# A two-layer streaming trunk on one core: gating values moved ahead of the pooling and kept in DRAM, system stores moved from ACT to SP

## The chip, the core and the metric

The kernel runs on one core of a Trainium2 chip, in one launch. A core has a matrix engine (TensorE, PE in the profile), a vector engine (VectorE, DVE), an activation engine (ScalarE, ACT), a general engine (GpSimd, POOL) and a sync engine (SyncE, SP), each with its own instruction stream that runs in order; they meet at semaphores. SP and ACT issue the transfers here. The metric is the device time of one execution in microseconds (us); lower is better.

## What is computed

Two layers with the same structure, for a prompt of 1024 tokens and eight sample requests of 16 tokens, 1152 tokens in all. In each layer one projection of the normalised tokens feeds four branches of 256 channels, and the gated branches go through an output projection that is added to the tokens:

```
x <- x + W_out[ silu(gates) * concat(A, B, C, D) ]      (all inputs from W_in @ rmsnorm(x))
A: time mixing   s = s*w_t + (s @ -kk_t)(kk_t*a_t) + v_t k_t ;  y_t = s @ r_t     (4 heads of 64)
B: latent attention with a rotary key and a block-causal mask
C: u * (W_s @ layer_norm(v) + b), W_s lower triangular, over chunks of 128 positions
D: trailing means over windows of 2, 4, 8, 16, minus the token, a linear map per group
```

The normalised v of the sample tokens (branch C) is one of the outputs, vn_o.

## The kernel before

The tokens stand in three groups of 384 columns. A layer is a row of projection blocks of 128 output channels: 24 for the inputs (F_ORDER) and 8 for the output. One block is 72 matmuls of 128x128 by 128x384: for each token group, eight parts of the input times three products (each factor is split into a high and a low part, xh, xl and wh, wl). The names in F_ORDER are the blocks: WDAD, K, R, V feed branch A, D and GD the pooling and its gate, VC and U the gating branch's values and inputs, GC its gate, Q, Q1K, CK the attention, GB and GA the other gates. Index 0 or 1 is the half of the 256 channels.

The weights of a block come in four pieces of 128 KB, issued by SP (line 238, wr, three buffers), copied to a high part by ACT (241) and a low part by POOL (242), in eight buffers each, so the weights of one block are made while the block before it runs. Each group's result lies in one of two pj buffers of PSUM until a sink on ACT and DVE has taken it (lines 383 to 400 for the blocks of branch A: scale, shift by one token, and for the third group the last columns into sho).

Beside the blocks run lanes: generators that put their instructions between the block's matmuls at fixed places (tick). Lane a holds the time mixing. For each half and token group, elementwise work gives keys and decays (kb, ar; 437 to 494). systems() (506 to 519) makes for each of 18 chunks of 64 tokens a triangular system: eight small matmuls into b, a mask on DVE into one of two ns buffers, and a store to DRAM (517). The chunks 16 and 17 hold the samples. solve() (522 to 555) loads all systems, chunks on partitions, and inverts them by forward substitution on DVE: 15 steps for the samples, then 31 for the prompt's halves, two operations a step (540, 542), with a last copy (552). It stores the inverses to dds and dd. recurrence() then takes the chunks in the order 16, 17, 0 to 15; prepare() loads a chunk's inverse into tt (571, 573), makes its products gm (582), and advance() carries the state S (678, 679). When six chunks are done, groupnorm (lane n; gn buffers, 730 to 752) begins. Lane v holds the norms of the gating values: for each of nine chunks of 128 tokens a pair of transposes into one of two st buffers of PSUM (850), statistics (852, 854), a scaling on DVE (857) and two operations on POOL (858, 859). m is a pool of eight tiles of 128 by 1152, gn has three buffers of 128 by 384.

The order on each engine is not that of the code: the framework's list scheduler sets it, from the program's dependences and its own costs, for each engine once; the hardware then follows it in order.

Of the kernel before, what the change touches and what calls it, by code (L numbers as in the profile page):

```python
# [10 lines left out]
F32 = mybir.dt.float32  # L11
F32R = mybir.dt.float32r
AF = mybir.ActivationFunctionType
ALU = mybir.AluOpType
# [17 lines left out]
(WDAD, K0, R0, V0, K1, R1, V1, D0, GD0, D1, GD1, VC0, VC1, U0, GC0, U1, GC1,  # L32
 GB0, GB1, Q0, Q1K, CK, GA0, GA1) = range(NF)

F_ORDER = (WDAD, K0, K1, R0, R1, V0, V1, D0, GD0, D1, GD1, VC0, VC1, U0, GC0, U1, GC1,
           Q0, Q1K, CK, GB0, GB1, GA0, GA1)


# [10 lines left out]
def tile_trunk(ctx: ExitStack, tc: tile.TileContext, *aps):  # L49
# [275 lines left out]
    def whole(t, c, cols):  # L325

        return t[2 * c:2 * c + 2, 0:128 * cols].rearrange("x (s t) -> x s t", s=64)

    def diagonal(t, i, n, cols, first=0):

        v = t[:, 0:128 * cols].rearrange("h (s i t) -> h s i t", s=64, i=2)[:, 0:n, i, first:first + n]
        step = n * (2 * cols + 1)
        assert v.ap[0][0] == step * (64 // n)
        return bass.AP(v.tensor, v.offset, [(step, t.shape[0] * 64 // n), v.ap[1], v.ap[2]])
# [10 lines left out]
    for l in range(L):  # L345
# [162 lines left out]
        def systems(g):  # L508
            for cl in range(6):
                c = 6 * g + cl  # L510
                pn = pb()[:, 0:128].rearrange("p (i t) -> p i t", i=2)
                for h in range(4):
                    mm(pn[hp(h), h // 2, :], KB[h // 2][g][hp(h), cl, h % 2, :], AR[h // 2][g][hp(h), cl, 0, :])
                ns = chp.tile([128, 2, 64], F32, tag="u0", name=nm("ns"), bufs=2)
                mk = cm[:, C_MP if c < 16 else C_MS, 0:64]
                V.tensor_tensor(out=ns, in0=pn, in1=mk.unsqueeze(1).broadcast_to([128, 2, 64]), op=ALU.mult)
                A.dma_start(out=whole(nd, c, 64) if c < 16 else whole(nds, c - 16, 64),
                            in_=ns.rearrange("p i t -> p (i t)"))
                if cl % 2:
                    yield  # L520

        def solve():
            NT = m_tile(1024).rearrange("p (s t) -> p s t", s=32)
            DT = m_tile(1024).rearrange("p (s t) -> p s t", s=32)
            sol = m_tile(768)
            TM = sol[:, 0:256]
            NTs = sol[:, 256:512].rearrange("p (s t) -> p s t", s=16)
            DTs = sol[:, 512:768].rearrange("p (s t) -> p s t", s=16)
            for i in range(2):
                SY.dma_start(out=NT[64 * i:64 * i + 64], in_=diagonal(nd, i, 32, 64))  # L530
                SY.dma_start(out=NTs[16 * i:16 * i + 16], in_=diagonal(nds, i, 16, 64))

            def invert(NTt, DTt, n, np_):
                full = DTt[0:np_]
                Po.memset(full, 0.0)
                Po.memset(full.rearrange("p s t -> p (s t)")[:, 0:n * n:n + 1], 1.0)
                for s in range(n - 1):
                    w = n - 1 - s
                    tm = TM[0:np_, 0:(s + 1) * w].rearrange("p (j t) -> p j t", t=w)
                    V.tensor_tensor(out=tm, in0=full[:, 0:s + 1, s:s + 1].broadcast_to([np_, s + 1, w]),  # L540
                                    in1=NTt[0:np_, s:s + 1, s + 1:n].broadcast_to([np_, s + 1, w]), op=ALU.mult)
                    V.tensor_tensor(out=full[:, 0:s + 1, s + 1:n], in0=full[:, 0:s + 1, s + 1:n], in1=tm, op=ALU.add)  # L542
                    if s % 3 == 2:
                        yield

            yield from invert(NTs, DTs, 16, 32)
            for i in range(2):
                A.dma_start(out=diagonal(dds, i, 16, 64), in_=DTs[16 * i:16 * i + 16])
            yield
            yield from invert(NT, DT, 32, 128)  # L550
            DN = NT
            V.tensor_copy(out=DN, in_=DT.rearrange("p s t -> p t s"))
            for i in range(2):
                A.dma_start(out=diagonal(dd, i, 32, 128), in_=DT[64 * i:64 * i + 64])
                A.dma_start(out=diagonal(dd, i, 32, 128, 64), in_=DN[64 * i:64 * i + 64])


        Sst = {}
# [266 lines left out]
            inproj(fg, sink_gd)  # L825


        def gating():
            sg = m_tile(1024)
            sgb = sg[:, 0:512].rearrange("p (a i t) -> p a i t", a=2, i=2)  # L830
            SY.dma_start(out=sgb, in_=sgub[l])
            sgg = sg[:, 512:1024].rearrange("p (a t) -> p a t", a=2)
            SY.dma_start(out=sgg, in_=sgugb[l])
            vraw = []
            for fv in (VC0, VC1):
# [3 lines left out]
                    A.activation(out=vr[:, gcols(g)], in_=ps, func=AF.Copy)  # L839
                inproj(fv, sink_v)  # L840
                vraw.append(vr)
            vn = [m_tile(1024), m_tile(1024), m_tile(1024)]

            def vnt(j):
                return vn[j // 4][:, (j % 4) * 256:(j % 4 + 1) * 256]

            def normalise(j):
                ps = st()[:, 0:256]
                for i in range(2):
                    PE.transpose(ps[:, i * 128:(i + 1) * 128], vraw[i][:, j * 128:(j + 1) * 128], ident)  # L850
                bs = smp.tile([128, 6], F32, tag="bs", name=nm("bs"))
                V.bn_stats(out=bs, in_=ps)
                mv = smp.tile([128, 2], F32, tag="mv", name=nm("mv"))
                V.bn_aggr(out=mv, in_=bs)
                rs = smp.tile([128, 1], F32, tag="rs1", name=nm("rs1"))
                rsqrt(rs, mv[:, 1:2], 1.0, ELN)
                V.tensor_scalar(out=vnt(j), in0=ps, scalar1=mv[:, 0:1], scalar2=rs, op0=ALU.subtract, op1=ALU.mult)
                Po.tensor_tensor(out=vnt(j), in0=vnt(j), in1=sgg[:, 0], op=ALU.mult)
                Po.tensor_tensor(out=vnt(j), in0=vnt(j), in1=sgg[:, 1], op=ALU.add)

            def norms():
                for j in range(9):
                    normalise(j)
                    if j % 2:
                        yield
                A.dma_start(out=vn_o[l], in_=vnt(8))
            go("v", norms())
            wst = m_tile(1024).rearrange("p (a h t) -> p a h t", a=2, h=4)
            SY.dma_start(out=wst[:, 0], in_=wsT[l])
            SY.dma_start(out=wst[:, 1], in_=wsS[l])  # L870
# [5 lines left out]
            for i, (fu, fg) in enumerate(((U0, GC0), (U1, GC1))):  # L876
# [2 lines left out]
                def sink_u(g, ps, u=u):  # L879
                    A.activation(out=u[:, gcols(g)], in_=ps, func=AF.Copy)  # L880
                inproj(fu, sink_u)
                finish("v")

                def sink_gc(g, ps, i=i, u=u):
                    t = silu(ps)
# [21 lines left out]
        def after_k1(g, zs):  # L907
            start("a", a_elem(1, g, zs))
            if g > 0:
# [2 lines left out]
        project([(l, WDAD), (l, K0)], xh, xl,  # L912
                [shift_sink(WDAD, lambda g: z6[:, gcols(g)], tanh_part),
                 shift_sink(K0, lambda g: zk0[:, gcols(g)], lambda g, zs: start("a", a_elem(0, g, zs)))])
        shifted(K1, lambda g: zk1[:, gcols(g)], after_k1)
        go("a", idle(4))
        go("a", systems(2))
        go("a", idle(4))
        go("a", solve())
        receptance(0, R0)  # L920
        receptance(1, R1)
        values(V0)
        values(V1)
        A.dma_start(out=shift_o[l], in_=sho)
        pool_in(0, D0)
        go("a", recurrence())
        pool_gate(0, GD0)
        pool_in(1, D1)
        pool_gate(1, GD1)
# [675 lines left out]
```

## Time and profile before

| | us |
|---|---|
| median of three runs | 1441.29 |
| lowest, highest | 1440.91, 1446.11 |
| profiled execution, its own time | 1443.43 |
| its span in the trace | 1441.6 |
| PE busy | 1357.0 |
| DVE, ACT, POOL busy | 779.5, 747.8, 466.8 |

The mean granted clock of the profiled execution is 0.988 of full speed. PE's idle times are read as rows "who waited, for whom, how long"; a busy share says nothing of which wait matters. In the stage around the change the blocks of layer 0 lie, in the span's time, as follows: K1 from 68.6 us, R0 from 90.1, R1 from 113.3, V0 from 129.6, V1 from 144.4, D0 from 159.3, GD0 from 173.8 to 205.0, VC0 and VC1 from 260 to 314, U0 from 314.1 to 348.0. The first system's matmul is at 90.0 us and the solve's first operation at 141.5; in layer 1 these are at 801.9 and 851.3.

### The profile page before, as it was taken

How to read it: one execution, taken by the hardware profiler on the slowest of the kernel's cores; microseconds unless marked ns; L12 is line 12 of the kernel's file. 1: busy time of each engine (PE TensorE's matmuls, PEld its weight loads, DVE VectorE, ACT ScalarE, POOL GpSimd, SP SyncE). 2: the span in 40 equal slices, each digit the busy share in tenths (PEclk: the TensorE clock that was granted, in tenths of full speed). 3: DMA queues.
4: the chain of work that ended last, by engine and by line, in shares of the span. 5: the costliest groups of instructions: out<-in, count | busy, mean ns of one | idle time of the engine just before them, and what ended most of it. 6: DMA issues, size and time to landing. Idle time of an engine off the chain costs nothing.

```text
span 1441.6 us, 26906 instructions
## 1 busy us (share of the span) xinstructions
PE 1357.0 (94%) x9962; PEld 1157.6 (80%) x9962; DVE 779.5 (54%) x1758; ACT 747.8 (52%) x2013; POOL 466.8 (32%) x600
## 2 busy tenths in 40 slices
PE   4799989999999998999989998999999999899999
PEld 3678878888988886679977788788789788766998
DVE  6875954435235567752287858444532375777211
ACT  6762234655466677652257621555653676766210
POOL 4514404426411023232162333332653111422320
PEclk9899999999999999999999999999999999999999
DMA  7212241210211213033300123321122111131222
GB/s 222 53 34 70 67 101 42 65 46 25 92 50 65 66 37 118 15 103 106 93 29 30 47 67 68 89 70 50 32 73 68 53 58 58 47 101 45 76 93 77
DMA packets 116596, 97.40 MB, mean 68 GB/s; under 512 B 46129, under 2 KB 111345, under 8 KB 116465
## 3 DMA queue, kind: packets, MB, share of 16 engines
q1 hardware_dynamic: 76776, 73.74, 17.8%
q10 hardware_dynamic: 39688, 21.94, 5.1%
q8 instruction: 79, 1.29, 0.4%
q14 instruction: 53, 0.43, 0.1%
HBM read 71.48 MB, written 24.16 MB: 66 GB/s over the span
## 4 chain that ended last, share of the span: by engine, by line
PE 67%; DVE 17%; DMA 5%; ACT 4%; issue 3%; POOL 3%; SPq 0%; ACTq 0%; DVEq 0%; POOLq 0%
PE pj L76 40%; PE b L76 14%; PE st L76 8%; DMA nd<-ns 3%; PE pj L1306 3%; DVE ea L278 2%; DVE m L540 2%; DVE m L542 2%; DMA tt<-dd 1%; POOL sp L99 1%; PE b L588 1%; DVE gn L730 1%; DVE ea L170 1%; DMA m<-nds 1%; DVE m L793 1%
## 5 line engine op out<-in xcount | busy, mean ns | idle before, releaser
L76 PE MATMUL pj<-xh,wh 128*128 128x384 f32 x1152 | 415.1, 361 | 19.3 <-ACT xh L280 7.3
L76 PE MATMUL pj<-xl,wh 128*128 128x384 f32 x1152 | 395.6, 343 | 3.8 <-POOL xl L282 2.8
L76 PE MATMUL pj<-xh,wl 128*128 128x384 f32 x1152 | 395.7, 344 | 0.0
L242 POOL TENSOR_TENSOR wl<-wr,wh 128x256 fp32r<-128x256 f32 x200 | 159.4, 805 | 459.6 <-ACT wh L241 398.0
L76 PEld LDWEIGHTS pj<-xh,wh 128*128 128x128 f32 x1152 | 220.9, 192 | 44.4 <-ACT sho L400 13.5
L76 PEld LDWEIGHTS pj<-xl,wh 128*128 128x128 f32 x1152 | 221.1, 192 | 12.1 <-POOL xl L282 4.8
L76 PEld LDWEIGHTS pj<-xh,wl 128*128 128x128 f32 x1152 | 220.6, 192 | 4.3 <-issue 3.1
L76 PE MATMUL pj<-yh,wh 128*128 128x384 f32 x384 | 129.3, 337 | 2.4 <-DVE x L1428 2.4
L76 PE MATMUL pj<-yh,wl 128*128 128x384 f32 x384 | 128.6, 335 | 0.0
L76 PE MATMUL pj<-yl,wh 128*128 128x384 f32 x384 | 128.3, 334 | 0.0
L241 ACT ACTIVATE wh<-wr 128x256 fp32r<-128x256 f32 x200 | 81.3, 414 | 80.7 <-PE pj L76 38.7
L242 POOL TENSOR_TENSOR wl<-m,wh 128x256 fp32r<-128x256 f32 x56 | 43.5, 789 | 102.8 <-ACT wh L241 84.9
L76 PEld LDWEIGHTS pj<-yh,wh 128*128 128x128 f32 x384 | 72.1, 188 | 3.7 <-DVE x L1428 2.7
L76 PEld LDWEIGHTS pj<-yl,wh 128*128 128x128 f32 x384 | 72.1, 188 | 0.1
L76 PEld LDWEIGHTS pj<-yh,wl 128*128 128x128 f32 x384 | 72.1, 188 | 0.1
L1295 ACT ACTIVATE X<-b,ng 128x512 f32<-128x512 f32 (+3 forms) x96 | 55.0, 577 | 25.6 <-DVE ng L1287 21.4
L76 PE MATMUL b<-sp,cr 128*128 128x384 f32 (+3 forms) x192 | 59.5, 385 | 3.2 <-POOL sp L99 2.8
L1283 DVE TENSOR_REDUCE mx<-b 128x1 f32<-128x512 f32 (+3 forms) x96 | 53.0, 555 | 9.7 <-PE b L76 8.0
L76 PEld LDWEIGHTS st<-X,X 128*64 128x64 f32 x576 | 35.1, 136 | 27.4 <-ACT X L1313 7.6
L1424 DVE TENSOR_TENSOR pt<-pj,pt 128x384 f32<-128x384 f32 x24 | 13.4, 557 | 80.6 <-PE pj L76 80.6
L241 ACT ACTIVATE wh<-m 128x256 fp32r<-128x256 f32 x56 | 22.2, 412 | 60.9 <-PE pj L76 59.2
L1306 PE MATMUL pj<-cm,X 128*128 128x128 f32 x288 | 48.0, 286 | 5.2 <-ACT X L1295 5.2
(307 smaller groups left out, 2584.9 us busy)
## 6 DMA issues: line engine op xcount, KB each, us to landing
wr<-in_win_dram SPq DMA_DIRECT2D x176, 128.0 KB
m<-in_wout_dram SPq DMA_DIRECT2D x12, 512.0 KB
x<-in_xT_dram SPq DMA_DIRECT2D x12, 384.0 KB
ysp<-m ACTq DMA_DIRECT2D x24, 192.0 KB
pt<-in_xT_dram SPq DMA_DIRECT2D x24, 192.0 KB
ea<-ysp SPq DMA_DIRECT2D x24, 192.0 KB
x1d<-x ACTq DMA_DIRECT2D x24, 192.0 KB
pt<-x1d SPq DMA_DIRECT2D x24, 192.0 KB
```

The source lines that it names most:

```text
L76: return PE.matmul(out, lhsT=lhsT, rhs=rhs, start=start, stop=stop, skip_group_check=True)
L99: by[1].tensor_tensor(out=view(lo), in0=src, in1=view(hi.bitcast(F32)), op=ALU.subtract)
L170: V.tensor_tensor(out=acc, in0=acc, in1=q, op=ALU.add)
L241: A.activation(out=h, in_=r, func=AF.Copy)
L242: Po.tensor_tensor(out=lo, in0=r, in1=h.bitcast(F32), op=ALU.subtract)
L278: V.scalar_tensor_tensor(out=t, in0=xs[k // 2][:, k % 2, :], scalar=vcs[:, l, V_NG + k:V_NG + k + 1], in1=rs, op0=ALU.mult, op1=ALU.mult)
L540: V.tensor_tensor(out=tm, in0=full[:, 0:s + 1, s:s + 1].broadcast_to([np_, s + 1, w]), in1=NTt[0:np_, s:s + 1, s + 1:n].broadcast_to([np_, ...
L542: V.tensor_tensor(out=full[:, 0:s + 1, s + 1:n], in0=full[:, 0:s + 1, s + 1:n], in1=tm, op=ALU.add)
L588: PE.transpose(pt[:, i * 128:(i + 1) * 128], KB[i][g][:, cl].rearrange("p a t -> p (a t)"), ident)
L1283: V.tensor_reduce(out=mx[:, b:b + 1], in_=pc[:, :w], axis=AX.X, op=ALU.max)
L1295: A.activation(out=P[:, :w], in_=pc[:, :w], func=AF.Exp, scale=SCALE, bias=ng, accum_out=sums[pr][:, b, s, h:h + 1])
L1306: PE.transpose(ptp[:, j * 128:(j + 1) * 128], Pb[slot][:, j * 128:(j + 1) * 128], ident)
```

## The change

Six edits, the same in both layers. The block order becomes WDAD, K0, V0, K1, V1, R0, R1, VC0, VC1, D0, GD0, D1, GD1, U0 and so on. The projection of VC0 and VC1 and their norms go into a function of their own, gating_values(), ahead of D0. A normalised chunk lies in one of the three gn buffers instead of an m tile, and SP stores it to a DRAM tensor vnd (and the ninth to vn_o as well, which ACT stored before); gating() loads vnd back ahead of U0 in three loads. The recurrence is queued behind VC1 and the norms, with four empty ticks between, and no longer behind D0. The wait for lane v moves from behind U0 to the start of gating(). The stores of the systems (18 a layer) and of the inverses (2 and 4) are issued by SP instead of ACT.

```diff
@@ -32,7 +32,7 @@
 (WDAD, K0, R0, V0, K1, R1, V1, D0, GD0, D1, GD1, VC0, VC1, U0, GC0, U1, GC1,
  GB0, GB1, Q0, Q1K, CK, GA0, GA1) = range(NF)
 
-F_ORDER = (WDAD, K0, K1, R0, R1, V0, V1, D0, GD0, D1, GD1, VC0, VC1, U0, GC0, U1, GC1,
+F_ORDER = (WDAD, K0, V0, K1, V1, R0, R1, VC0, VC1, D0, GD0, D1, GD1, U0, GC0, U1, GC1,
            Q0, Q1K, CK, GB0, GB1, GA0, GA1)
 
 
@@ -514,7 +514,7 @@
                 ns = chp.tile([128, 2, 64], F32, tag="u0", name=nm("ns"), bufs=2)
                 mk = cm[:, C_MP if c < 16 else C_MS, 0:64]
                 V.tensor_tensor(out=ns, in0=pn, in1=mk.unsqueeze(1).broadcast_to([128, 2, 64]), op=ALU.mult)
-                A.dma_start(out=whole(nd, c, 64) if c < 16 else whole(nds, c - 16, 64),
+                SY.dma_start(out=whole(nd, c, 64) if c < 16 else whole(nds, c - 16, 64),
                             in_=ns.rearrange("p i t -> p (i t)"))
                 if cl % 2:
                     yield
@@ -545,14 +545,14 @@
 
             yield from invert(NTs, DTs, 16, 32)
             for i in range(2):
-                A.dma_start(out=diagonal(dds, i, 16, 64), in_=DTs[16 * i:16 * i + 16])
+                SY.dma_start(out=diagonal(dds, i, 16, 64), in_=DTs[16 * i:16 * i + 16])
             yield
             yield from invert(NT, DT, 32, 128)
             DN = NT
             V.tensor_copy(out=DN, in_=DT.rearrange("p s t -> p t s"))
             for i in range(2):
-                A.dma_start(out=diagonal(dd, i, 32, 128), in_=DT[64 * i:64 * i + 64])
-                A.dma_start(out=diagonal(dd, i, 32, 128, 64), in_=DN[64 * i:64 * i + 64])
+                SY.dma_start(out=diagonal(dd, i, 32, 128), in_=DT[64 * i:64 * i + 64])
+                SY.dma_start(out=diagonal(dd, i, 32, 128, 64), in_=DN[64 * i:64 * i + 64])
 
 
         Sst = {}
@@ -825,11 +825,11 @@
             inproj(fg, sink_gd)
 
 
-        def gating():
-            sg = m_tile(1024)
-            sgb = sg[:, 0:512].rearrange("p (a i t) -> p a i t", a=2, i=2)
-            SY.dma_start(out=sgb, in_=sgub[l])
-            sgg = sg[:, 512:1024].rearrange("p (a t) -> p a t", a=2)
+        vnd = dr.tile([9, 128, 256], F32, tag=f"vnd{l}", name=nm("vnd"))
+
+        def gating_values():
+
+            sgg = m_tile(512).rearrange("p (a t) -> p a t", a=2)
             SY.dma_start(out=sgg, in_=sgugb[l])
             vraw = []
             for fv in (VC0, VC1):
@@ -839,10 +839,6 @@
                     A.activation(out=vr[:, gcols(g)], in_=ps, func=AF.Copy)
                 inproj(fv, sink_v)
                 vraw.append(vr)
-            vn = [m_tile(1024), m_tile(1024), m_tile(1024)]
-
-            def vnt(j):
-                return vn[j // 4][:, (j % 4) * 256:(j % 4 + 1) * 256]
 
             def normalise(j):
                 ps = st()[:, 0:256]
@@ -854,17 +850,35 @@
                 V.bn_aggr(out=mv, in_=bs)
                 rs = smp.tile([128, 1], F32, tag="rs1", name=nm("rs1"))
                 rsqrt(rs, mv[:, 1:2], 1.0, ELN)
-                V.tensor_scalar(out=vnt(j), in0=ps, scalar1=mv[:, 0:1], scalar2=rs, op0=ALU.subtract, op1=ALU.mult)
-                Po.tensor_tensor(out=vnt(j), in0=vnt(j), in1=sgg[:, 0], op=ALU.mult)
-                Po.tensor_tensor(out=vnt(j), in0=vnt(j), in1=sgg[:, 1], op=ALU.add)
+                t = s_tile("gn", 3, 256)
+                V.tensor_scalar(out=t, in0=ps, scalar1=mv[:, 0:1], scalar2=rs, op0=ALU.subtract, op1=ALU.mult)
+                Po.tensor_tensor(out=t, in0=t, in1=sgg[:, 0], op=ALU.mult)
+                Po.tensor_tensor(out=t, in0=t, in1=sgg[:, 1], op=ALU.add)
+                SY.dma_start(out=vnd[j], in_=t)
+                if j == 8:
+                    SY.dma_start(out=vn_o[l], in_=t)
 
             def norms():
                 for j in range(9):
                     normalise(j)
                     if j % 2:
                         yield
-                A.dma_start(out=vn_o[l], in_=vnt(8))
             go("v", norms())
+
+        def gating():
+            finish("v")
+            sgb = m_tile(512).rearrange("p (a i t) -> p a i t", a=2, i=2)
+            SY.dma_start(out=sgb, in_=sgub[l])
+            vn = []
+            for a in range(3):
+                n = min(4, 9 - 4 * a)
+                vn.append(m_tile(1024))
+                SY.dma_start(out=vn[a][:, 0:256 * n].rearrange("p (j t) -> p j t", j=n),
+                             in_=vnd[4 * a:4 * a + n].rearrange("j p t -> p j t"))
+
+            def vnt(j):
+                return vn[j // 4][:, (j % 4) * 256:(j % 4 + 1) * 256]
+
             wst = m_tile(1024).rearrange("p (a h t) -> p a h t", a=2, h=4)
             SY.dma_start(out=wst[:, 0], in_=wsT[l])
             SY.dma_start(out=wst[:, 1], in_=wsS[l])
@@ -879,7 +893,6 @@
                 def sink_u(g, ps, u=u):
                     A.activation(out=u[:, gcols(g)], in_=ps, func=AF.Copy)
                 inproj(fu, sink_u)
-                finish("v")
 
                 def sink_gc(g, ps, i=i, u=u):
                     t = silu(ps)
@@ -912,18 +925,20 @@
         project([(l, WDAD), (l, K0)], xh, xl,
                 [shift_sink(WDAD, lambda g: z6[:, gcols(g)], tanh_part),
                  shift_sink(K0, lambda g: zk0[:, gcols(g)], lambda g, zs: start("a", a_elem(0, g, zs)))])
+        values(V0)
         shifted(K1, lambda g: zk1[:, gcols(g)], after_k1)
         go("a", idle(4))
         go("a", systems(2))
         go("a", idle(4))
         go("a", solve())
+        values(V1)
         receptance(0, R0)
         receptance(1, R1)
-        values(V0)
-        values(V1)
         A.dma_start(out=shift_o[l], in_=sho)
+        gating_values()
+        go("a", idle(4))
+        go("a", recurrence())
         pool_in(0, D0)
-        go("a", recurrence())
         pool_gate(0, GD0)
         pool_in(1, D1)
         pool_gate(1, GD1)
```

The order of instructions changes between the end of K0 and GC1 in each layer. On DVE, layer 0, before: the solve's last operations for the prompt, and behind them the masks (gm) and the recurrence's first sums. L540 and L542 are the solve, L793 is the pooling, u_380 the recurrence.

```order
L793 SCALAR_TENSOR_TENSOR m_1713<-pt_1846,pinv_t,zsm_1714 64x128
L542 TENSOR_TENSOR m_1390<-m_1390,m_1391 128x29x3
L582 TENSOR_TENSOR gm_1866<-b_1867,cm 128x256
L540 TENSOR_TENSOR m_1391<-m_1390,m_1389 128x60
L582 TENSOR_TENSOR gm_1866<-b_1871,cm 128x256
L542 TENSOR_TENSOR m_1390<-m_1390,m_1391 128x30x2
L540 TENSOR_TENSOR m_1391<-m_1390,m_1389 128x31
L542 TENSOR_TENSOR m_1390<-m_1390,m_1391 128x31
L552 COPY m_1389<-m_1390 128x1024
L657 TENSOR_TENSOR u_380_1950<-b_1952,u_380_1950 128x128
```

The same place after the change: the norms (L848 to L854 of the changed file) stand behind the copy, the masks behind the first norms.

```order
L540 TENSOR_TENSOR m_1502<-m_1501,m_1500 128x31
L542 TENSOR_TENSOR m_1501<-m_1501,m_1502 128x31
L552 COPY m_1500<-m_1501 128x1024
L848 BN_STATS bs_1939<-st_1936 128x6
L848 BN_STATS bs_1954<-st_1951 128x6
L850 BN_AGGR mv_1941<-bs_1939 128x2
L850 BN_AGGR mv_1956<-bs_1954 128x2
L854 TENSOR_SCALAR gn_1946<-st_1936,mv_1941,rs_379_1943 128x256
L854 TENSOR_SCALAR gn_1961<-st_1951,mv_1956,rs_384_1958 128x256
L848 BN_STATS bs_1978<-st_1975 128x6
```

Nothing stands between the solve's 62 large operations any more; before, sinks, pooling and masks did.

On PE, layer 0, after the change, inside D0's first group (pj_1926): the transposes of the second, third and fourth norm (L846) with projection matmuls between. Nine matmuls of D0 and the first norm's two transposes stand ahead of this piece.

```order
L846 MATMUL st_1951<-cm,m_1660 128x128
L846 MATMUL st_1951<-cm,m_1818 128x128
...
L76 MATMUL pj_1926<-xh_190,wl_1807 128x384
L846 MATMUL st_1975<-cm,m_1660 128x128
L846 MATMUL st_1975<-cm,m_1818 128x128
L76 MATMUL pj_1926<-xh_190,wh_1806 128x384
L76 MATMUL pj_1926<-xl_191,wh_1806 128x384
L846 MATMUL st_1990<-cm,m_1660 128x128
L846 MATMUL st_1990<-cm,m_1818 128x128
```

Before, D0 held no norm; the transposes stood in U0. The third norm needs the st buffer of the first.

On SP, layer 0, after the change: system stores (L517) and weight loads (L238) in turn; wr_1299 belongs to R1, wr_1430 to wr_1466 to VC0.

```order
L517 DMA nd_79_312<-ns_1122 2x64x128
L517 DMA nd_79_312<-ns_1130 2x64x128
L238 DMA wr_1299<-in_win_dram 128x256
L517 DMA nd_79_312<-ns_1213 2x64x128
L238 DMA wr_1430<-in_win_dram 128x256
L517 DMA nd_79_312<-ns_1221 2x64x128
L238 DMA wr_1442<-in_win_dram 128x256
L517 DMA nd_79_312<-ns_1245 2x64x128
L238 DMA wr_1454<-in_win_dram 128x256
L517 DMA nd_79_312<-ns_1253 2x64x128
```

Before, SP held only the weight loads here, and the stores stood on ACT between sinks and weight copies.

## Rows read from the trace of the kernel before

**Rows 1.** The page: busy us (share of the span) and instructions of each engine.
```profile
PE 1357.0 (94%) x9962; PEld 1157.6 (80%) x9962; DVE 779.5 (54%) x1758; ACT 747.8 (52%) x2013; POOL 466.8 (32%) x600
```

**Rows 2.** PE's waits, 67.2-380, then 781-1083: total us, times, longest.
```profile
PE pj L76 <- ACT sho L400: 3.6, 2, 2.0
PE b L76 <- DVE m L540: 2.8, 1, 2.8
PE b L76 <- DVE S L679: 2.8, 2, 1.9
PE st L850 <- DVE m L857: 1.8, 1, 1.8
PE pj L76 <- DVE m L540: 1.6, 1, 1.6
PE b L76 <- DVE m L668: 1.5, 2, 1.3
PE b L76 <- DMA tt<-dd: 1.1, 1, 1.1
...
PE b L76 <- DVE m L542: 3.0, 1, 3.0
PE pj L76 <- ACT sho L400: 2.6, 2, 2.0
...
PE b L76 <- DVE m L668: 1.5, 2, 1.2
```

**Rows 3.** Window: busy by engine, PEclk, DMA; PE's timeline: start, us.
```profile
186.10:189.50 3.40, 3.40 (x12) 3.40 (x12) 0.99 (x1) 0.00 (x0) 0.00 (x0) 0.50 0.62 92
...
141.14 0.33 PE L76 MATMUL pj<-xh,wl 128*128 128x384 f32 x1
...
142.18 0.33 PE L76 MATMUL pj<-xh,wl 128*128 128x384 f32 x1
```

**Rows 4.** Timelines of PE and DVE; then PE's groups 90 to 125.
```profile
83.93 0.91 PE L76 MATMUL st<-ea,cr 128*128 128x384 f32 x2
...
91.18 1.97 DVE L484 TENSOR_TENSOR kb<-ea,ea 64x384 f32<-64x384 f32 x2
...
L76 PE MATMUL b<-ar,kb 64*64 64x64 f32 x144 | 7.5, 227 | 1.3 <-DVE ns L516 0.7 <-DVE kb L484 0.6
```

**Rows 5.** DVE's timeline, the first and last of seven ns operations.
```profile
118.67 0.29 DVE L516 TENSOR_TENSOR ns<-b,cm 128x128 f32<-128x128 f32 x1 [1.20 <-DMA nd<-ns]
...
129.86 0.29 DVE L516 TENSOR_TENSOR ns<-b,cm 128x128 f32<-128x128 f32 x1 [0.33 <-DMA nd<-ns]
```

**Rows 6.** SP's waits, 90 to 200: us in total, times, longest.
```profile
SPq L238 <- POOL wl L242: 54.1, 20, 18.3
```

**Rows 7.** The chain that ended last, 110 to 142: start, us, what.
```profile
115.08 0.49 ACTq L517
...
131.69 3.77 DMA nds<-ns
...
136.51 4.86 DMA m<-nds
```

**Rows 8.** The solve's window, and its two large groups on DVE.
```profile
141.50:187.10 45.60, 39.09 (x277) 36.71 (x277) 42.97 (x120) 10.08 (x29) 17.55 (x25) 0.99 0.23 57
...
L540 DVE TENSOR_TENSOR m<-m,m 128x31 f32<-128x31 f32 (+15 forms) x31 | 13.9, 447 | 0.8
L542 DVE TENSOR_TENSOR m<-m,m 128x31 f32<-128x31 f32 (+15 forms) x31 | 13.1, 423 | 0.8
```

**Rows 9.** DVE's timeline inside the solve: two of its operations.
```profile
166.80 0.95 DVE L540 TENSOR_TENSOR m<-m,m 128x252 f32<-128x252 f32 x1
...
168.77 0.42 DVE L540 TENSOR_TENSOR m<-m,m 128x247 f32<-128x247 f32 x1
```

**Rows 10.** Tile st, 260-400: ns min/median/max, first and last start.
```profile
L852 DVE BATCH_NORM_STATS2 bs<-st x9: 416/432/433, 316.5 to 334.3; 128x6 f32<-128x256 f32 x9
L857 DVE TENSOR_SCALAR m<-st,mv,rs x9: 511/535/545, 318.5 to 336.8; 128x256 f32<-128x256 f32 x9
```

## The prediction

> **What bounds the kernel now.** I read the page's busy shares first, then TensorE's waits by what ended them, then the granted clock behind the long waits, and last the chain of waits. The busy shares show PE at 94% of the span and every other engine at 54% or less [rows 1]: a microsecond is won only where PE stands, or where it runs at the lower clock. Both kernels have the same 6,263 rows on PE, and up to the end of K0 and again from GC1 on they stand in the same order in each layer. So the sum is a sum over the waits between these points, some 67 to 380 us (layer 0) and 781 to 1083 us (layer 1).
>
> In that stretch the waits of layer 0 add up to 18.3 us: the rows shown give 15.2, the seven others 3.1. Those of layer 1 give 13.7: 7.1 shown, eleven others 6.6 [rows 2]. The reader is to see two kinds. The solve's kind: PE waits for sinks on ACT (L400) that stand behind system stores, for DVE's solve (L540, L542), and for the products behind it. The rest: norms (L857) in U0 and the recurrence's own chain (L668, L679, tt). Behind some of the long waits PE runs for 3.4 us at a granted clock of 0.50, the 1.2 GHz level. At full clock six projection matmuls take 1.04 us (141.14 to 142.18), 0.1735 each [rows 3]; at half of it half of 3.4 is lost: 1.7 us each time. Layer 0 has three such stretches inside the stage (186, 288, 326 us), layer 1 one (896 us).
>
> **What goes.** If every wait of the stage went with its slow stretch, layer 0 would win 18.3 + 3 x 1.7 = 23.4 us and layer 1 13.7 + 1.7 = 15.4 us. PE's own work does not change, and no matmul is removed. The nine stores and four loads a layer that are new (vnd, 1.1 MB each way) lie on SP and the DMA rings. They cost something only through whom they hold up.
>
> **What comes, step by step for layer 0.**
>
> *First systems.* Before, PE comes to the first b<-ar,kb at 90.0, behind K1's 72 matmuls and 6 small products; now 72 more matmuls (V0, 72 x 0.1735 = 12.5) and 3 more products of about 0.85 (0.91 in the row, overlapping a little) stand ahead: 105.0. The keys they need come later than that: between the product of cumulative decays (83.93) and the end of the key product (91.18 + 1.97) lie 9.2 us [rows 4]. The last such product needed stands 36 matmuls and two products ahead of the first system, so at 97.1, and the keys at 106.3. New wait 1.3 us (0 if DVE is less crowded, 4 if more).
>
> *System stores.* The two ns buffers pace this chain: DVE's mask waits until the store before the last has landed. From 118.67 to 129.86 lie six intervals, 1.87 us each [rows 5]. Eighteen systems then take from 107.3 to 107.3 + 17 x 1.87 = 139.1. Moving the issue from ACT to SP frees ACT's sinks, which held PE 3.6 and 2.6 us. It does not shorten the landing. On SP six weight loads now stand between the stores, and a weight load is where SP usually stands (54.1 us in 20 waits, the longest 18.3) [rows 6]. I give this 1.0 us; below zero it can be by one or two if issue on ACT was late, above by 8. The weights behind the stores are VC0's and are not wanted before some 155 us, so PE does not starve there.
>
> The Trainium skill, "DMA: Bandwidth & Descriptors", section "Issuing engines are not separate DMA queues", says that DMAs started by different engines run on the same DMA engines and that spreading them saves only the time of issuing. By it the stores land as before, as my 1.87 has it. If they came at the rate of the issues instead, about 0.5 us by the issue on ACT [rows 7], the chain would be 17 x 1.4 = 23 us shorter, and the larger gain below would be the likeliest. The landings of the last stores [rows 7] speak for the rule.
>
> *Solve.* From the last ns to the first L540 there lie 10.0 us before: store 3.8, issue of the load, load 4.9 [rows 7]. So the solve starts at about 139.1 + 1.0 + 10.0 = 150.1. It took 45.6 us from its start to the end of the copy (L552), with DVE 43.0 busy: its 62 large operations 27.0, the 30 small ones 7.6, the copy 1.1 [rows 8]. The other 7.3 us were sinks, pooling and mask operations (L387 to L397, L793, L582, L350 to L354); in the new order only R1's sinks and five tiny ones lie between, 2.9. Its operations run up to twice as long in places (0.95 against 0.42) [rows 9], there beside work on POOL, and POOL was busy 17.55 of the 45.6 us; beside VC0 and VC1 it has little but eight weight copies. I take 2 us off for that (0 to 4). 45.6 - 7.3 + 2.9 - 2.0 = 39.2, so the copy ends at 189.3. The norms stand right behind it on DVE: two statistics, two aggregates, the root on ACT, and the first scaling, 2 x 0.43 + 2 x 0.17 + 0.4 + 0.53 = 2.1 [rows 10]. The first st buffer is free at 191.4.
>
> *PE meanwhile.* From the first system to the third norm's transpose in D0.0 PE has 381 projection matmuls (66.1), the 144 system products (7.5) [rows 4], three small products (2.5) and four transposes (1.1); with 0.2 a block for what blocks lose at their ends, 1.0: 106.3 + 78.2 = 184.5. It stands there, or earlier at R1's sinks, which wait behind the first solve step: 6.9 us in all (0 to 14). I count one slow stretch of 1.7 behind it (0 to two). In layer 1 the path from the first system to the solve was 2.1 us shorter (801.9 to 851.3, against 90.0 to 141.5), so 4.8 us there.
>
> *Norms after the third.* The nine norms in U0 cost PE one wait of 1.8 [rows 2]; now seven follow in D0 with three to eighteen other matmuls between: I take 2.5 (0 to 8). Each result is in one of three gn buffers until SP has stored it, and the recurrence's L730 uses the same three; the first stores find SP free of weights that are due, so I leave it in these bounds.
>
> *Recurrence.* It keeps its chain, now in D0 to U1. Its waits were 6.3 us in layer 0 (L679 2.8, L668 1.5, tt 1.1, two smaller 0.9) and 3.2 in layer 1. The tt wait goes, since the inverse is stored some 10 us ahead of the first prompt chunk: 5.2 and 3.0 remain (3 to 9). PE does not come to b<-vu,gm behind the solve any more: that wait (2.8 and 3.0) is the one now standing in D0.0. U0's norm wait and its slow stretch are gone.
>
> *The sum.* Layer 0: 1.3 + 6.9 + 1.7 + 2.5 + 5.2 = 17.6 against 23.4, so -5.8. Layer 1: 1.3 + 4.8 + 1.7 + 2.5 + 3.0 = 13.3 against 15.4, so -2.1. Together -7.9: 1443.4 (profiled run) becomes 1435.5. That run stood 2.1 over the median of 1441.3, so I forecast 1433.4, a gain of 0.55%. Its own range, with 3 us either way in each layer, is 1427 to 1440. What a measurement here can tell from no change is 0.5%, 7.2 us; the forecast stands just beyond that.
>
> **Rivals.**
>
> *Larger gain: the solve is done before PE wants it.* If stores or solve run 7 us faster than I count, the 6.9 and 4.8 and their slow stretches vanish, and the norms, with DVE free, cost 1. Layer 0: 23.4 - (1.3 + 1 + 5.2) = 15.9; layer 1: 15.4 - (1.3 + 1 + 3.0) = 10.1. Time 1441.3 - 26.0 = 1415.3. For it: the solve runs alone on DVE, and 25 us of VC0 and VC1 ask nothing of DVE. Against it: V0 now stands ahead of the first system, and the landings stay.
>
> *Slower: SP holds the system stores behind weight loads.* A store that is ready waits until POOL has freed a weight buffer; two ns buffers then stop DVE, and the whole chain of systems, loads and solve comes later, while PE's work in front of D0.0 stays. Each microsecond is one more of standing at the third norm. From 4.0 us a layer on the gain is gone (7.9 / 2); at 8 us a layer the time is 1433.4 + 16 = 1449.4. For it: SP's longest wait of 18.3 us at such a load, and six of them between the stores. Against: PE's first twelve systems come within 16 us, and the weights there are R1's and VC0's, whose buffers come free while V1 runs.
>
> *No change: the waits only move.* PE is 94% busy and its work is the same. If DVE is as late at D0.0, the norms and chunk 16 as it was at V0, V1, D0 and GD0, each layer's new waits are 3 us larger than in my sum: 1439. For it: layer 1, where little was to be won.
>
> **How the numbers follow.** Forecast 0.43, larger gain 0.18, no change 0.19, slower 0.20. Of the forecast's own range about 0.6 lies below 1434.1, so faster by over 0.5%: 0.18 + 0.26 = 0.44; within it: 0.17 + 0.19 = 0.36; slower: 0.20. With all terms at their good ends the time would be near 1409, at their bad ends above 1465; eight in ten I put at 1419 to 1451, which cuts the far half of the larger gain and the far end of the slow case.
>
> **What will show it.** Right if PE has no wait at ACT sinks (L400) in V0 and V1, none at b<-vu,gm, and its longest new wait stands at the norm transposes in D0.0, 4 to 9 us, ended by DVE's scaling (L854), with the solve's copy ending between 186 and 193 us and the solve starting between 147 and 153. The systems are right if ns intervals stay near 1.9 us and SP's stores are held by landings, not by weights. The steps on the recurrence are right if the waits at S and at the L668 products add up to 3 to 6 us a layer. The forecast is wrong if the copy comes ahead of PE's D0.0 (larger gain), if SP's waits at weight loads lie between the stores and the solve starts after 157 (slower), or if waits of over 3 us appear at the norms or at chunk 16 that DVE, POOL or the gn buffers end.

## The result: 0.65% slower, and the profile after

The changed kernel takes 1453.72 us (median of four runs, 1451.42 to 1457.32), against 1441.16 in four runs of the kernel before: 1.0065 times as long, 95% interval 1.0045 to 1.0086. The forecast was 1433.4 with a range of 1419 to 1451. The sign was wrong, and the time lies outside the range. The profiled execution took 1453.76 us, with a span of 1452.0 and a mean granted clock of 0.978 (before 1443.43, 1441.6 and 0.988).

The page's line of busy times, to be held against [rows 1]:

```profile
PE 1360.0 (94%) x9962; PEld 1165.2 (80%) x9962; DVE 786.2 (54%) x1758; ACT 747.0 (51%) x2013; POOL 464.5 (32%) x600
```

PE issues as many matmuls and is busy 3 us longer: it runs at the lower clock for longer. Two windows a kernel hold the stage from the end of K0 to the start of Q0, layer 0 and layer 1 (columns: start and end, us; busy us and count of PE, PEld, DVE, ACT, POOL; granted clock; DMA share; GB/s). Before:

```profile
62.80:394.70 331.90, 309.19 (x2771) 268.08 (x2771) 179.60 (x414) 156.47 (x470) 125.37 (x163) 0.97 0.22 60
781.30:1098.20 316.90, 302.89 (x2771) 262.93 (x2771) 174.99 (x404) 152.65 (x460) 124.43 (x161) 0.99 0.22 61
```

And after:

```profile
62.30:392.50 330.20, 307.94 (x2771) 270.61 (x2771) 182.66 (x414) 155.69 (x470) 124.57 (x163) 0.96 0.24 67
779.20:1107.40 328.20, 307.07 (x2771) 268.84 (x2771) 178.71 (x404) 152.51 (x460) 122.74 (x161) 0.96 0.24 66
```

Layer 0 gains 1.7 us, layer 1 loses 11.3; of the spans' difference of 10.4, 0.8 is left for everything outside the stages. PE's waits in the changed kernel, first 66.8 to 380, then 781 to 1105 (us in total, times, longest), to be held against [rows 2]; the 4.3 at L397 lies at the stage's very start and stands in both kernels:

```profile
PE st L846 <- DVE gn L854: 7.0, 1, 7.0
PE b L76 <- DVE m L397: 4.3, 1, 4.3
PE st L846 <- DVE mv L850: 3.4, 2, 3.1
PE b L76 <- DVE ns L516: 3.0, 2, 2.4
PE b L76 <- DVE u L657: 1.8, 2, 1.3
PE pj L76 <- ACT sho L400: 1.1, 1, 1.1
...
PE st L846 <- DVE gn L854: 9.8, 3, 7.1
PE b L76 <- DVE u L657: 4.6, 2, 3.3
PE b L76 <- DVE ns L516: 2.8, 2, 2.1
PE pj L76 <- ACT sho L400: 2.5, 2, 2.2
```

The reader is to see that the waits at the solve (L540, L542) and at L668 of [rows 2] are gone, and that fewer but longer waits stand in their place, in both layers alike. What they bring is seen when the timeline of PE (start, us, what, the idle time before it and what ended it) is laid beside the granted clock. All idle times of 2 us and more from the first systems to the end of the stage:

```profile
120.61 0.45 PE L76 MATMUL b<-ar,kb 64*64 64x64 f32 x8 [2.36 <-DVE ns L516]
191.16 0.66 PE L846 MATMUL st<-cm,m 128*128 128x128 f32 x2 [6.95 <-DVE gn L854]
214.02 0.66 PE L846 MATMUL st<-cm,m 128*128 128x128 f32 x2 [3.09 <-DVE mv L850]
...
832.57 0.45 PE L76 MATMUL b<-ar,kb 64*64 64x64 f32 x8 [2.10 <-DVE ns L516]
...
870.92 0.44 PE L76 MATMUL pj<-xh,wh 128*128 128x384 f32 x1 [2.18 <-ACT sho L400]
...
903.23 0.66 PE L846 MATMUL st<-cm,m 128*128 128x128 f32 x2 [7.12 <-DVE gn L854]
922.28 0.41 PE L846 MATMUL st<-cm,m 128*128 128x128 f32 x2 [2.33 <-DVE gn L854]
...
1017.91 0.97 PE L76 MATMUL b<-sp,cr 128*128 128x384 f32 x4 [3.34 <-DVE u L657]
```

The windows behind them (columns as above):

```profile
121.50:128.50 7.00, 6.31 (x26) 6.08 (x26) 2.59 (x9) 1.12 (x4) 0.73 (x1) 0.51 0.29 90
191.20:197.00 5.80, 5.80 (x21) 5.61 (x22) 2.65 (x8) 1.35 (x6) 5.41 (x9) 0.52 0.92 139
213.50:221.00 7.50, 6.98 (x47) 5.24 (x48) 4.65 (x11) 3.07 (x12) 5.28 (x8) 0.54 0.40 100
835.00:838.50 3.50, 3.50 (x13) 3.50 (x12) 1.30 (x5) 0.89 (x2) 0.74 (x1) 0.51 0.33 94
...
870.00:880.00 10.00, 9.08 (x52) 9.08 (x53) 9.12 (x31) 2.48 (x7) 3.42 (x4) 1.00 0.09 16
...
903.20:907.00 3.80, 3.77 (x14) 3.70 (x15) 2.10 (x6) 1.26 (x5) 3.64 (x5) 0.54 0.94 141
923.50:934.00 10.50, 10.16 (x72) 7.82 (x72) 5.61 (x16) 4.39 (x16) 6.15 (x10) 0.51 0.38 105
1019.00:1023.00 4.00, 4.00 (x40) 3.34 (x38) 1.38 (x4) 2.38 (x6) 2.05 (x2) 0.57 0.05 12
```

Behind seven of the eight waits PE runs 3.5 to 10.5 us near 0.5, the 1.2 GHz level; behind the one at ACT's sink (870.92) it keeps 1.00, the 2.4 GHz level. In the first of the two waits of 7 us the clock falls before the wait ends (0.68 in 184.00 to 191.00), and that part of the slow time costs nothing. To size the rest I took from each trace's rows PE's idle time and, as an estimate of the loss, half of its other time at the lower clock, from K0's end to GC1's end. (Half is a little too much: at the lower clock projection matmuls start every 0.32 us, 193.00 to 195.24, and at the higher one every 0.17.) "Rest" is the length of the stage's window less these two, PE's work at its full pace:

| us, layer 0 / layer 1 | idle | lost to the clock | rest |
|---|---|---|---|
| before | 22.7 / 14.0 | 8.4 / 1.7 | 300.8 / 301.2 |
| after | 22.3 / 21.1 | 10.9 / 10.2 | 297.0 / 296.9 |
| gating and stores, values as before | 20.6 / 16.1 | 1.7 / 3.4 | 300.3 / 298.8 |
| after, V0 alone put back | 18.8 / 15.0 | 6.5 / 5.0 | 300.1 / 299.2 |

In layer 1 idle time and clock cost 7.1 and 8.5 more than before, and the rest gives back 4.3: the 11.3 that the layer loses. The last two lines belong to experiments below.

### The profile page after: what moved, and what is told of

The parts are those of the page before. It is cut to its first block, busy times and chain, and to the rows that moved or that the text cites. A ratio compares the mean times of both kernels' runs of the same rounds, so it can differ in the third digit from the quotient of the medians.

```text
span 1452.0 us, 26966 instructions
## 1 busy us (share of the span) xinstructions
PE 1360.0 (94%) x9962; PEld 1165.2 (80%) x9962; DVE 786.2 (54%) x1758; ACT 747.0 (51%) x2013; POOL 464.5 (32%) x600
## 4 chain that ended last, share of the span: by engine, by line
PE 68%; DVE 16%; ACT 4%; DMA 4%; issue 3%; POOL 3%; SPq 0%; DVEq 0%; ACTq 0%; POOLq 0%
PE pj L76 40%; PE b L76 15%; PE st L76 9%; PE pj L1321 3%; DVE ea L278 2%; DVE m L540 2%; DVE m L542 2%; DMA nd<-ns 2%; POOL pt L786 1%; PE b L588 1%; DVE kb L489 1%; POOL sp L99 1%; DVE gn L730 1%; DMA m<-nds 1%; DVE xl L282 1%
```

## The experiments

The change has three parts: the blocks V0 and V1 behind K0 and K1 ("values"); the gating values and norms ahead of the pooling, kept in DRAM, with the recurrence behind them ("gating"); the stores on SP ("stores"). My first theory: the wait at the third norm and its slow clock cost the gain. The rivals: the stores on SP, the three gn buffers, or the place of the value blocks. Ratios are to the kernel before as run beside them (medians 1442.95 to 1443.88), with 95% intervals.

**Each part alone, and two by two.** The stores alone on the kernel before:

```diff
-                A.dma_start(out=whole(nd, c, 64) ...
+                SY.dma_start(out=whole(nd, c, 64) ...
-                A.dma_start(out=diagonal(dds, ... / diagonal(dd, ...
+                SY.dma_start(out=diagonal(dds, ... / diagonal(dd, ...
```

> The kernel before with one part of the change: system and inverse stores issued by SP. Theory A (the time went into TensorE standing at the norms behind the solve and the slow clock behind such waits, so it belongs to the gating part): no cost here, 1436 to 1443 us, the ACT waits at L400 (3.6 and 2.6 us) smaller. Rival B (SP holds the system stores behind weight loads, so the solve is late): 1446 to 1452, with the solve's first operation after 143 us (141.5 before).

Measured 1436.99, 0.9951 [0.9933, 0.9969]: faster by half a per cent. PE's waits at ACT sinks (L400) in layer 0 fall from 3.6 [rows 2] to 2.4. The values alone:

```diff
-F_ORDER = (WDAD, K0, K1, R0, R1, V0, V1, D0, ...
+F_ORDER = (WDAD, K0, V0, K1, V1, R0, R1, D0, ...
```

> The kernel before with one part of the change: V0 behind K0 and V1 behind K1. Theory A: within 4 us of before (1437 to 1445), since the recurrence still stands behind D0 and GD0 and the solve's path is only shifted. Rival C (V0 ahead of the first system delays systems and solve by its 12.5 us, and PE pays for it wherever the solve is wanted): 1447 to 1455, most of the loss at the first product behind the solve in GD0.

Measured 1460.52, 1.0117 [1.0088, 1.0146], above both ranges expected: the values' place alone is slower than the whole change. The gating alone (the change's diff without the other two):

```diff
-F_ORDER = (WDAD, K0, K1, R0, R1, V0, V1, D0, GD0, D1, GD1, VC0, VC1, U0, ...
+F_ORDER = (WDAD, K0, K1, R0, R1, V0, V1, VC0, VC1, D0, GD0, D1, GD1, U0, ...
```

> The kernel before with one part of the change: gating values and norms ahead of the pooling and kept in DRAM, recurrence behind them; V0, V1 and the stores of systems as before. Theory A: this part carries the loss, 1447 to 1456, with waits at the norm transposes in D0 and three or more stretches at half clock in each layer's D0 and GD0. Rivals B and C: 1436 to 1443.

Measured 1454.78, 1.0073 [1.0046, 1.0099]. The whole change with its stores on ACT again (the first diff turned round):

> The changed kernel with system and inverse stores issued by ACT again. Theory A: no gain, 1452 to 1460, the wait at the third norm's transpose still 5 to 9 us in each layer. Rival B: 1440 to 1447, and the solve's first operation before 148 us (150.3 in the changed kernel).

Measured 1456.76, 1.0089 [1.0065, 1.0113], in the first range, but not by the wait expected: at the norms PE waits 1.4 at most. Its longest wait in layer 0 is at VC's sinks, which stand on ACT behind the inverse stores:

```profile
PE pj L76 <- ACT m L839: 8.5, 1, 8.5
```

**Against the wait itself.** Each with one edit to the changed kernel. The norms begun fourteen ticks later:

```diff
+            go("v", idle(14))
             go("v", norms())
```

> The changed kernel with 14 empty ticks ahead of the norms, so that their transposes stand behind D0 and the first chunk, from GD0's second group on. Theory A (TensorE stands at the third norm behind the solve and then runs at half clock): the waits of 7.0 and 7.1 us and the one of 3.1 go, with the slow stretches behind them; at the end of D0 the solve has just ended, so 0 to 2 us come back. About 10 us a layer less: 1430 to 1438. Rival D (whatever stands behind the solve is late, the waits only move to the first chunk's products and to norms beside the recurrence): 1450 to 1457.

Measured 1467.53, 1.0156 [1.0122, 1.019], above both ranges. The wait at the third norm is gone and another has its place, for the load of the first state S: its m tile comes free only when an inverse store has landed, and the load stands on SP behind weight loads.

```profile
PE b L76 <- DMA m<-in_S_dram: 6.3, 1, 6.3
```

The wait filled with 30 matmuls:

```diff
+                if j == 2:
+                    fill = pb()
+                    for _ in range(30):
+                        mm(fill[:, :G], HALVES, xh[0][:, 0, :])
```

> The changed kernel with 30 projection-size matmuls, whose result nobody reads, on TensorE right ahead of the third norm's transpose: 5.2 us of work a layer inside a wait of 7. If the slow clock behind the wait is a cost of its own (theory A): the wait falls to about 2 us, the stretch at half clock behind it goes, and the kernel gets faster though it does more, by 2 to 3 us a layer: 1448 to 1451. If only the wait counts (rival E): the time stays, 1452 to 1455. If the wait weren't there to be filled: 1464.

Measured 1454.82, 1.0076 [1.0049, 1.0103], the time of the changed kernel within the intervals. PE's timeline: the third norm's idle time falls from 6.95 to 2.25.

```profile
191.12 1.11 PE L850 MATMUL st<-cm,m 128*128 128x128 f32 x4 [2.25 <-DVE gn L858]
```

The clock in the 3.8 us behind it (columns as above) still lies near the lower level, where the changed kernel showed 5.8 us at 0.52:

```profile
191.20:195.00 3.80, 3.76 (x14) 3.55 (x15) 1.85 (x6) 1.15 (x5) 2.97 (x5) 0.55 0.88 132
```

So PE had room for 5 us more work a layer, and keeping it busy there wins nothing that can be told: the wait ends at the same time (191.12, 191.16 before), set by the solve and not by PE's idle time in front of it. The gn buffers replaced by two of the norms' own:

```diff
...
-                t = s_tile("gn", 3, 256)
+                t = sgt[:, 512 + 256 * (j % 2):768 + 256 * (j % 2)]
```

> The changed kernel with two buffers of their own for the normalised values (free columns of the tile that holds the norms' scale and shift) instead of the three gn buffers that the recurrence and the group norm use too. If the stores of vnd hold up the scalings (theory F: the second wait of 3.1 us in layer 0 ended 0.7 us after a scaling that had waited for such a store): 3 to 6 us a layer less, 1442 to 1448. Theory A without F: the wait at the third norm stays at 6 to 8 us and the time within 3 us of the changed kernel, 1451 to 1457.

(sgt is the tile of the norms' scale and shift, made wider.) Measured 1460.05, 1.011 [1.0074, 1.0145], above both ranges, the waits at the norms longer (longest 8.2). Two buffers stand here in place of three, so this does not settle what the sharing costs; it shows only that buffers of their own at this price win nothing.

**The parts in pairs.** On the kernel before, only the system stores (L517) on SP:

> The kernel before with only the 18 system stores a layer on SP; the six inverse stores stay on ACT. With all of them on SP the kernel before ran at 1437.0, with a wait for the reloaded inverse (tt<-dd) of 1.4 and 3.0 us that was 1.1 and 0.2 before. If the inverse stores on SP cause that wait (they stand behind weight loads): it falls back to under 1.2 in both layers and the time to 1432 to 1436. If not: 1436 to 1440.

Measured 1437.9, 0.9958 [0.9943, 0.9973]: the inverse stores add nothing that can be told. Gating and stores, values as before:

> The kernel before with two parts of the change: gating values and norms ahead of the pooling (with the recurrence behind them), and the stores on SP; V0 and V1 at their old place. If the parts add (gating alone cost 0.73% of the time, the stores on SP won 0.49%): 1443 to 1448. If stores and reloads on SP get into each other's way (SP then carries system, inverse and vnd stores): 1449 to 1456. If the stores on SP win more where PE stands at the norms behind the solve: 1436 to 1442.

Measured 1439.01, 0.9963 [0.995, 0.9977]. This is the changed kernel without the move of the values, and it is 14.7 us faster than it. Its windows of the stage, and one in the place of the first long slow stretch (columns as above):

```profile
63.20:385.80 322.60, 302.00 (x2770) 262.78 (x2771) 181.99 (x414) 155.28 (x469) 124.25 (x163) 0.99 0.26 68
770.50:1088.80 318.30, 302.19 (x2772) 263.03 (x2771) 178.31 (x404) 152.57 (x461) 123.40 (x161) 0.99 0.26 68
...
121.50:128.50 7.00, 7.00 (x54) 6.68 (x53) 2.70 (x10) 2.48 (x6) 3.40 (x6) 1.00 0.17 51
```

The layers lie 7.6 and 9.9 us under the changed kernel's (this profiled execution, 1434.09, was itself 4.9 under its median). Values and stores:

> The kernel before with two parts of the change: V0 and V1 behind K0 and K1, and the stores on SP. If the parts add (values alone cost 1.17%, the stores won 0.49%): 1450 to 1455. If the cost of the values' place was ACT standing at the stores (waits at L400 in R0 and R1 of 2.2 and 2.7 us): 1438 to 1445.

Measured 1469.49, 1.0178 [1.0152, 1.0204], above both ranges and the slowest of all. Without the gating's work between, PE comes to the recurrence before the inverse is stored:

```profile
PE b L76 <- DMA tt<-dd: 7.3, 2, 6.2
PE b L76 <- DVE gm L582: 5.4, 1, 5.4
```

**Which value block.** The changed kernel with only V0 put behind R1:

```diff
-F_ORDER = (WDAD, K0, V0, K1, V1, R0, R1, VC0, ...
+F_ORDER = (WDAD, K0, K1, V1, R0, R1, V0, VC0, ...
...
-            vfm.append(v)
+            vfm.insert(0 if fv == V0 else len(vfm), v)
```

(The second edit keeps the list of the two halves in its order.)

> The changed kernel with V0 behind R1 again (K0, K1, V1, R0, R1, V0, VC0, ...); V1 stays behind K1. If V0 in front of the first system makes the solve late (theory G): the first system comes at 88 to 91 us instead of 100.4, the solve's copy at 174 to 179 instead of 188.0, the wait at the third norm falls from 7.0 to under 2.5 us, and the time is 1436 to 1442. If it is V1's place (theory H): 1449 to 1456.

Measured 1438.71, 0.9966 [0.9948, 0.9984]: the whole loss is gone. The changed kernel with only V1 put there:

```diff
+F_ORDER = (WDAD, K0, V0, K1, R0, R1, V1, VC0, ...
```

> The changed kernel with V1 behind R1 again (K0, V0, K1, R0, R1, V1, VC0, ...); V0 stays behind K0. Theory G: no better than the changed kernel, 1449 to 1458, the wait at the third norm 5 to 9 us. Theory H: 1436 to 1443.

Measured 1455.59, 1.0089 [1.0064, 1.0115]: nothing is won. Two rows for each kernel show why: first and last start of the small products into b (the systems are the first of them), and of the solve's copy (layer 0 to layer 1). The changed kernel:

```profile
L76 PE MATMUL b<-ar,kb x152: 218/218/373, 100.4 to 198.6; 64*64 64x64 f32 x144, 64*128 64x128 f32 x8
...
L552 DVE COPY m<-m x2: 1036/1036/1036, 188.0 to 900.0; 128x1024 f32<-128x1024 f32 x2
```

With V0 back:

```profile
L76 PE MATMUL b<-ar,kb x152: 218/218/579, 90.0 to 196.3; 64*64 64x64 f32 x144, 64*128 64x128 f32 x8
...
L552 DVE COPY m<-m x2: 1119/1124/1128, 176.5 to 880.4; 128x1024 f32<-128x1024 f32 x2
```

In layer 0 the systems begin 10.4 us earlier, and the copy 11.5 us. PE's wait at the third norm is 2.27 in place of 6.95. Gating and stores without the values' move have 88.7 and 175.2. With V1 back they stand at 101.8 and 189.0, and the wait is 6.28. So my first theory named an effect: the wait at the third norm and its slow clock follow from the place of V0.

**Improvements tried.** The recurrence one or two ticks later on the kernel before with system stores on SP (`go("a", idle(1))`, then `idle(2)`, ahead of it):

> The kernel before with the 18 system stores on SP (1437.9 so far) and the recurrence one tick later. The wait at b<-vu,gm behind the solve (3.0 and 3.1 us) has 9 matmuls more in front of it: 1.5 us less in each layer, and if the slow stretch behind the wait goes with it 1.7 more: 1431 to 1436. If the first chunk's products just wait elsewhere: 1437 to 1440.

> The same with the recurrence two ticks later: about 25 matmuls (4.3 us) more in front of b<-vu,gm, but its masks now stand behind the solve's copy on DVE (1.9 us later). The wait falls to under 1.5 us in each layer: 1430 to 1436 with the slow stretch gone; 1437 to 1442 if the later recurrence is missed at its end (GC0, U1).

Measured 1455.0, 1.0078 [1.0054, 1.0102], and 1449.27, 1.0037 [1.0025, 1.005]. Both failed, above every range expected; the second has a new wait of 7.1 at ACT's vu (L597). On the version with gating and stores, the inverse stores back on ACT (`SY` to `A` at dds and dd), and then the norms' own two buffers as above:

> Gating ahead and system stores on SP (1439.0 with V0 and V1 at their old place), with the six inverse stores on ACT. The wait for the reloaded inverse (1.2 us in layer 0) goes: 1435 to 1439. If the inverse stores on ACT hold its sinks at the norms: 1440 to 1445.

> Gating ahead and all stores on SP, V0 and V1 at their old place, with two buffers of their own for the normalised values instead of the three gn buffers. If the waits at the norms (2.3 and 1.6, 2.2 and 1.0 us) come from stores of vnd that hold gn buffers: 1432 to 1437. If two buffers are fewer than three in effect (beside the late solve they cost 6 us): 1440 to 1446.

Measured 1449.61, 1.0047 [1.003, 1.0065], and 1439.93, 0.9979 [0.9967, 0.9991]. The first lies above both its ranges, the second between its two. The first puts 10.6 us back, with PE again at VC's sink:

```profile
PE pj L76 <- ACT m L839: 2.7, 1, 2.7
```

Five versions beat the kernel before: the stores alone (1436.99), the system stores alone (1437.9), the change with V0 back (1438.71), and gating with stores (1439.01, or 1439.93 with own buffers). Their intervals overlap, so it is not shown that any of the others beats the stores alone.

## Why the prediction was wrong, step by step

*Right, in part by luck: the solve's timing in layer 0.* The last ns was foreseen near 140 and stands at 141.2; the solve starts at 150.3 (150.1 foreseen), its copy ends at 189.0 (189.3), the third norm's wait is 6.95 (6.9) and ends at 191.16 (191.4). The step on the systems came out by two errors that cancel: they begin at 100.4, not 106.3 (no wait of PE for the keys shows), and their pace is 2.22 us each, not 1.87. Tile ns, before and in the changed kernel:

```profile
L516 DVE TENSOR_TENSOR ns<-b,cm x18: 259/291/293, 94.2 to 131.4; 128x128 f32<-128x128 f32 x18
...
L516 DVE TENSOR_TENSOR ns<-b,cm x18: 278/291/293, 103.4 to 141.2; 128x128 f32<-128x128 f32 x18
```

(141.2 - 103.4) / 17 = 2.22. Before it was (131.4 - 94.2) / 17 = 2.19: my 1.87 was read from six of the seventeen intervals, and these were shorter than the rest. PE's way to the third norm cancels likewise: it comes there at 184.2 (184.5 foreseen), having begun 5.9 us earlier and taken 83.8 us, not 78.2. The wait at b<-vu,gm behind the solve is gone, as foreseen. (The new loads of vnd are three a layer, not four; no term rests on that.)

*Wrong, and decisive: the slow stretches.* I counted one of 1.7 us a layer. The loss to the clock is 10.9 and 10.2, where it was 8.4 and 1.7 (I had seen 5.1 of the 8.4). By my sum it would have fallen by 3.4 in layer 0 and stayed in layer 1; it rose by 2.5 and 8.5. I had priced each of the smaller waits at its idle time alone: the systems' 1.3, the norms' 2.5, the recurrence's 5.2. In each, one wait is 2.1 to 3.3 us long in one layer or both, and behind each of these PE runs 3.5 to 10.5 us near half its clock. This step is off by 5.9 us in layer 0 and 8.5 in layer 1. With it the account closes: from the forecast's -7.9 to the spans' +10.4 are 18.3 us, of which the clock makes 14.4, the waits 11.2 (2.0 and 9.2) and the time outside the stages 0.8, less 8.1 in the rest.

*Wrong: layer 1's waits.* My terms for them add up to 11.6 us without the clock; measured at the same places are 2.8 (systems, 1.3 foreseen), 7.1 (third norm, 4.8), 2.7 (later norms, 2.5), 2.5 (ACT's sinks, none) and 4.6 (recurrence, 3.0), together 19.7. The 4.8 rested on layer 1's shorter path before. Now the path from the first system to the copy's end is as long in layer 1 as in layer 0, 88.5 (812.6 to 901.1) against 88.6 (100.4 to 189.0). My own sign of being wrong came as well: waits of over 3 us at the norms that DVE ends, after the third one's too (3.09 at 214.02).

*Right: no loss at the system stores on SP.* That mechanism was my rival on the slower side, and it is refuted: the stores on SP are the best part of the change, 0.49% alone. SP's waits, 95 to 260 us, in the changed kernel:

```profile
SPq L238 <- POOL wl L242: 48.7, 20, 10.5
...
SPq L517 <- DVE ns L516: 14.7, 12, 2.7
```

SP stands at the stores for ns, so weights do not hold them. The Trainium skill, "DMA: Bandwidth & Descriptors", section "Issuing engines are not separate DMA queues", has it that another issuing engine saves only the issue. The pace of the ns agrees in the changed kernel (2.22 against 2.19); with the stores alone it is (128.4 - 94.3) / 17 = 2.01, and what made it shorter there is not shown. What is won lies on ACT, where a store that is not ready holds the weight copies and sinks behind it. ACT's waits for ns, 90 to 200 us, kernel before:

```profile
ACT wh L241 <- DVE ns L516: 5.5, 3, 2.9
ACT gn L383 <- DVE ns L516: 3.7, 1, 3.7
```

With the stores on SP, alone or in the changed kernel, ACT has none of these. Between gating with its stores on ACT (1454.78) and on SP (1439.01) lie 15.8 us, 10.6 of them the inverse stores'.

*The rival that was missing: the place of V0.* I worked the change out as one and found the 12.5 us of V0 ahead of the systems payable, since PE's wait at the third norm came to 6.9. That wait came as foreseen; what else the late chain costs, the slow clock and the longer waits at the other places, was not in the sum. Ahead of the first system V0's 72 matmuls put the whole chain back by 10 to 13 us (100.4 against 90.0 and 88.7; 188.0 against 176.5 and 175.2); behind R1 they are work for PE while DVE solves. Beside the other two parts the values' place costs 14.7 us, and V0 alone explains all of it (1438.71 with V0 back, 1439.01 with both). It is no fixed price: with the stores on ACT, gating with the values moved takes 1456.76 and without 1454.78, a difference that the intervals do not resolve.

*Wrong: the gating part wins nothing.* Alone it is 0.73% slower, and with the stores it takes 1439.01 where the stores alone take 1436.99. In that version PE's idle time is 20.6 and 16.1 us, against 22.7 and 14.0 before: in sum the waits moved and did not go, as my rival of no change had it. The lower loss to the clock in its line of the table comes from the fastest of its nine executions.

*Open.* Filling a wait left a shorter wait and a slow stretch, so it is not shown how idle time and clock hang together one by one. Nor is it shown why PE's "rest" is some 4 us lower a layer after the change, nor why the values' place costs little beside gating with the stores on ACT.

## What to carry to other kernels

Price a change that has separable parts part by part, each against the chain it lies on: here one part gained, one gained nothing, and one block's place cost more than the first had won. Where one engine bounds the kernel, try the work of that engine that nobody waits for yet behind the start of a long chain on other engines, not in front of it. Give each wait that appears its slow stretch as well, and keep stores that wait for data off an engine that has sinks to serve.

## What was not expected of the hardware

Behind seven of the changed kernel's eight waits of 2.10 to 7.12 us the granted clock was near 0.5, but not behind 2.18 at 870.92; and the version with gating and stores waits 2.34 us at 192.03 and keeps 1.00 from 190 to 200, while with V0 back a wait of 2.27 at the same norm (193.32) stands in 3.5 us at 0.51 (193.0 to 196.5). So the idle time alone doesn't say whether the clock falls. Nor does it say for how long: 10.5 us behind 2.33 (922.28), where chunk 16's small products and few projection matmuls run, 3.8 behind 7.12 (903.23), where the clock had fallen during the wait (0.77 in 896.0 to 903.2).
